# Two of the four weight sums of each gate/up pair of the second feed-forward made by an accumulating transfer

## The chip, the cores and the metric

The kernel runs on one core of a Trainium2 chip. The core has TensorE (PE in the profile; PEld is its weight load), VectorE (DVE), ScalarE (ACT), GpSimd (POOL) and SyncE (SP). Each takes its own list of instructions in a fixed order and waits on semaphores that others raise. Transfers between HBM and the on-chip memory are issued here from the lists of SyncE and GpSimd, and they run on 16 DMA engines that both share. The metric is the time of one execution on the device, in microseconds (us).

## The reference

One layer on 512 tokens of width 1024, all in float32: a SwiGLU feed-forward of width 2816, a merge of two token mixers (dilated attention and a gated linear recurrence), and a second SwiGLU feed-forward, each with an RMS norm before and after it. What matters here is the second feed-forward:

```
def swiglu(x, w_gate, w_up, w_down):
    return (jax.nn.silu(x @ w_gate) * (x @ w_up)) @ w_down
...
f = swiglu(rms_norm(h, ffn2_norm_pre[l]), ffn2_w_gate[l], ffn2_w_up[l], ffn2_w_down[l])
h = h + 0.5 * rms_norm(f, ffn2_norm_post[l])
```

## The kernel before

**Precision.** Every float32 operand is split into a high and a low part (`split`: ScalarE copies the rounded value, L302; VectorE subtracts it from the original, L303). A product is then three matmuls: high by high, high by low, low by high.

**Seven products instead of eight.** The 22 blocks of 128 gate and 128 up columns are numbered f. Those with f of 3 and more in the second feed-forward treat gate and up together as a two by two block matrix and multiply it with a two by two split of the activations in Strassen's manner, with seven products p1 to p7 instead of eight. The weights come as four pieces u0, u1, g0 and g1 of 128 rows by 512. `w_forms` makes four sums from them on VectorE: s2 = u0 + u1 (L691), s1 = s2 + g0 (L692), u0 + g0 (L693) and s1 + g1 (L696). Then it splits four tiles: a holds g0 and g1 (p1, p2), b holds s1 and s2 (p6, p5), c holds u0 + g0 and u1 (p7, p4), and d holds the last sum (p3).

**Order of the products.** Pairs 3 and 4 go through `seven` (copies on line L836), whose products follow each other as p1, p2, p6, p5, p7, p4, p3. Its accumulators are read out on the way: p1 is copied out (c1 below) before p6 accumulates on top of it, and that sum is copied out (c6) before p7 accumulates on top of that. The gate output of the first half (g0 below, L841) is read on VectorE before p4 reuses its bank. From pair 5 on, `seven_on` takes p1, p5, p6, p2, p7, p3, p4 (copies on L743). One product is 12 matmuls.

**Order of the whole.** `ffn_order` prepares the weights of pair f + 1 ahead of the products of pair f (`prep`, with a priority raised by AHEAD = 100). Between pairs it places parts of the down product (`prepd` for its weights, `down7` for its matmuls, L1043 to L1045), which is done in seven products too. A planner decides the order of the list of each engine from priorities and its own costs. Once built, the lists are fixed, and an instruction that waits holds up everything behind it in its list.

**Buffers.** Raw weights land by SyncE (L242) in a ring of four tiles of 512 KB (`raw`). Split weights use four tiles (`w8`) and two small ones (`w4`). The sums s1 and s2 share one tile under the tag `s`, of which there are two. Just ahead of the first pair both `s` tiles hold differences of the activations (`ts`, L667 and L668). The first of these is free once p5's activation form is split from it (`big<-ts`). The second is changed in place later (L673), and is free once p4's form is split from it (also `big<-ts`).

```
            DVE.tensor_add(s2, u0, u1)
            DVE.tensor_add(s1, s2, g0)
            DVE.tensor_add(u0, u0, g0)
            a, b, c, d = w8(), w8(), w8(), w4()
            split(a[:, 0, :], a[:, 1, :], gr)
            DVE.tensor_add(g1, s1, g1)
            split(b[:, 0, :], b[:, 1, :], s12.rearrange("p s c -> p (s c)"))
            split(c[:, 0, :], c[:, 1, :], ur)
            split(d[:, 0, :], d[:, 1, :], g1)
```

Of the kernel before, what the change touches and what calls it, by code (L numbers as in the profile page):

```python
# [10 lines left out]
F32 = mybir.dt.float32  # L11
F32R = mybir.dt.float32r
AF = mybir.ActivationFunctionType
ALU = mybir.AluOpType
AX = mybir.AxisListType

P = 128
T = 512
D = 1024
KC = D // P  # L20
NF = 22
FF_PARTS = ((0, 4), (4, 8), (8, 12), (12, 16), (16, 22))
NSTD = {1: 6, 2: 3}

SEVEN = range(4)
STEPS_AT = {1: ((6, 7, 7, 8), range(9, 13), range(13, 17), range(17, 21)),
# [5 lines left out]
RAW_W = 1024  # L32
# [3 lines left out]
AHEAD = 100  # L36
# [29 lines left out]
def ffn_order(n):  # L66

    order = [("std", f) for f in range(NSTD[n])]  # L70
    after = {}
# [3 lines left out]
    ready = False  # L75
    for f in range(NSTD[n], NF):
        if not ready:
# [83 lines left out]
def stream_groups():  # L161

    groups, cur, w = [], [], 0
    for key, width in stream_plan():
        if w + width > RAW_W or (cur and cur[0][0][0] == "start"):
            groups.append(cur)
            cur, w = [], 0
        cur.append((key, w, width))
        w += width
    groups.append(cur)  # L170
    return groups
# [12 lines left out]
def hybrid_layer(ctx: ExitStack, tc: tile.TileContext, xT: bass.AP, xN: bass.AP, wst: bass.AP,  # L184
                 first: bass.AP, rows: bass.AP, consts: bass.AP, bias: bass.AP, out: bass.AP):
    nc = tc.nc
    DVE, ACT, PE = nc.vector, nc.scalar, nc.tensor
# [3 lines left out]
    wpool = ctx.enter_context(tc.tile_pool(name="wpool", bufs=4))  # L191
# [39 lines left out]
    groups = stream_groups()  # L231
    state = {"g": 0, "i": 0, "off": 0, "raw": None, "ahead": AHEAD, "split": None}
# [21 lines left out]
    def raw_two(key, dst=None):  # L254

        return [raw_of(key + (n,), None if dst is None else dst[:, i * RAW_W:(i + 1) * RAW_W])
                for i, n in enumerate(("lo", "hi"))]

    def fetch(key, slot=None, ahead=0):

        with tc.high_priority(offset=ahead if slot else state["ahead"]):
            src = raw_of(key)
            w = src.shape[-1]
            t = slot() if slot else w8() if w > 512 else w4()
            split(t[:, 0, :w], t[:, 1, :w], src)
            return t[:, 0, :w], t[:, 1, :w]

    def w8():
        return wpool.tile([P, 2, 1024], F32R, name="w8", tag="w8", bufs=4)

    def w4():
        return wpool.tile([P, 2, 512], F32R, name="w4", tag="w4", bufs=2)
# [28 lines left out]
    def split(dh, dl, src):  # L301
        state["split"] = ACT.activation(dh, src, AF.Copy).ins  # L302
        state["low"] = DVE.tensor_sub(dl, src, dh.bitcast(F32)).ins  # L303
# [7 lines left out]
    def tmp(name):  # L311
        return tpool.tile([P, T], F32, name=name, tag="t")
# [17 lines left out]
    def gemm(ps, wt, x, sl=slice(0, T), ks=None):  # L330
        n = x.n
        a, b = k128(wt[0], n), k128(wt[1], n)
        for k in ks or range(n):
            mm3(ps, a[:, k, :], b[:, k, :], x.hi[k][:, sl], x.lo[k][:, sl], k == 0, k == n - 1)

    def gemm_first(keys, x, slots, then):


        wts = [fetch(k, None if i < 4 else slots.pop(0)) for i, k in enumerate(keys)]
        pss = [acc_ps() for _ in keys]  # L340
        for sl in HALVES:
            for i, (wt, ps) in enumerate(zip(wts, pss)):
                for k in range(x.n):
                    mm3(ps[:, sl], k128(wt[0])[:, k, :], k128(wt[1])[:, k, :], x.hi[k][:, sl],
                        x.lo[k][:, sl], k == 0, k == x.n - 1)
                if sl.start == 0:
                    for f in then.get(i + 1, ()):
                        f()
        return pss
# [95 lines left out]
    def gains(pool, *ids):  # L445

        t = pool.tile([P, 2, D], F32, name="gains", tag="wd", bufs=1)
        for j, i in enumerate(ids):
            nc.gpsimd.dma_start(t[:, j, :], bass.AP(tensor=rows.tensor, offset=rows.offset + i * D,
                                                    ap=[[0, P], [1, D]]))  # L450
        return t[:, 0, :], t[:, 1, :]
# [229 lines left out]

    spool = [None]

    def w_forms(key):

        with tc.high_priority(offset=AHEAD):
            ur, gr = raw_two(key)
            u0, u1, g0, g1 = (r[:, i * 512:(i + 1) * 512] for r in (ur, gr) for i in range(2))
            s12 = spool[0].tile([P, 2, 512], F32, name="s12", tag="s", bufs=2)
            s1, s2 = s12[:, 0, :], s12[:, 1, :]  # L690
# [9 lines that stand above are left out]
            lo, hi = slice(0, 512), slice(512, 1024)  # L700
            return {"p1": a[:, :, lo], "p2": a[:, :, hi], "p6": b[:, :, lo], "p5": b[:, :, hi],
                    "p7": c[:, :, lo], "p4": c[:, :, hi], "p3": d}
# [156 lines left out]
    def ffn(n, x, r, forms_x, apool, pss):  # L859
# [70 lines left out]
        def std_out(psg, psu, f):  # L930

            g = tmp("g")
            if r is None:
                ACT.activation(g, psg, AF.Silu)
                into(f, lambda dst, v: DVE.tensor_mul(dst, v(psu), v(g)))
                return
            u = tmp("u0")
            DVE.tensor_mul(g, psg, r)
            ACT.activation(g, g, AF.Silu)
            DVE.tensor_mul(u, psu, r)  # L940
            into(f, lambda dst, v: DVE.tensor_mul(dst, v(u), v(g)))
# [124 lines left out]

        keys = [(w, n, i) for i in range(NSTD[n]) for w in ("gate", "up")]
        forms = {}
        for ev in ffn_order(n):
            if ev[0] == "std":  # L1070
                j = ev[1]
                while len(pss) < 2 * j + 2:
                    pss.append(acc_ps())
                    gemm(pss[-1], fetch(keys[len(pss) - 1]), x)
                with tc.high_priority(offset=EVAC if j == NSTD[n] - 1 else 0):
                    std_out(pss[2 * j], pss[2 * j + 1], j)

                for step in steps[j:] if j == min(NSTD[n], 4) - 1 else steps[j:j + 1]:
                    step()
            elif ev[0] == "prep":  # L1080
                forms[ev[1]] = w_forms(("gu", n, ev[1]))
            elif ev[0] == "prepd":
                forms[ev[1:]] = d_forms(*ev[1:])
            elif ev[0] == "seeds":
                for g in groups(ev[2])[:3]:
                    seed(ev[1], *g)
            elif ev[0] == "down7":
                down7(*ev[1:], forms.pop(ev[1:]))
            else:
                prod(ev[1], forms.pop(ev[1]))  # L1090
# [9 lines left out]
    def spare(pool):  # L1100

        def of(t):
            return t[:, 0:4, :].rearrange("p (s k) t -> p s (k t)", s=2)

        return {"e": lambda: of(pool.tile([P, 8, T], F32R, name="act", tag="e", bufs=1)),
                "tt": lambda: of(pool.tile([P, 4, T], F32R, name="act", tag="tt", bufs=1)),
                "xf": lambda: of(pool.tile([P, 4, T], F32R, name="xf", tag="xf", bufs=4)),
                "tx": lambda: tx_slot(pool).rearrange("p s k t -> p s (k t)")}
# [15 lines left out]
    for k in range(KC):  # L1124
        wh, wl, raw = wts[k]
# [77 lines left out]
    with ExitStack() as mx:  # L1203
# [129 lines left out]
        def first_forms():  # L1333
            forms[order[0]] = w_forms(order[0])
# [5 lines left out]
        def pair_of(key):  # L1340

            i = order.index(key)
            if i + 1 < len(order):
                forms[order[i + 1]] = w_forms(order[i + 1])
            return forms.pop(key)
# [149 lines left out]
        for c in range(0, KC, 2):  # L1495
            g, u = tmp("g"), tmp("u")
# [12 lines left out]
    with ExitStack() as mx:  # L1509
# [183 lines left out]
        for c in range(KC):  # L1693
            if c < 3:
                ps = pss[c]
            else:
# [17 lines left out]
                 {(1, 3): lambda: (bd2.turn(0), bd2.turn(1))})  # L1714
    keys = [(w, 2, i) for i in range(NSTD[2]) for w in ("gate", "up")]
    pss = gemm_first(keys[:NFIRST], u2, [spare(ap2)["tx"]],
# [5 lines left out]
    grow5, _ = gains(ap2, 4)  # L1722
# [138 lines left out]
```

## Time and profile before

| what | value |
|---|---|
| median of 3 runs | 1209.24 us (1208.63 to 1209.45) |
| the profiled execution's own time | 1209.61 us |
| its span, first to last instruction | 1207.8 us |
| TensorE busy over the span | 1198.6 us (99%) |
| VectorE busy over the span | 1033.3 us (86%) |
| ScalarE busy over the span | 831.8 us (69%) |
| GpSimd busy over the span | 26.1 us (2%) |
| mean granted TensorE clock | 0.999 |
| pairs of the second feed-forward, from the first product of pair 3 | 898.55 us to about 1165 us |

All engine times in the text count from the start of the span of the profiled execution. A row of the timeline gives start, duration, engine, line, operation, and out<-in; behind it in brackets stands how long the engine had been idle before it, and what ended that. Matmuls overlap in their records: a matmul of 256 columns is shown as 0.28 us long, but the next one starts 0.12 us later. So a product of 12 matmuls takes 1.44 us. Transfers are shown with the time from issue to landing.

### The profile page before, as it was taken

Reading aid. Unit: us, or ns where it says so; the run is one execution under the profiler, and the core shown is the slowest. Engines: PE = TensorE matmul, PEld = TensorE weight load, DVE = VectorE, ACT = ScalarE, POOL = GpSimd, SP = SyncE. Lnnn points to the kernel's source line nnn. Section 1 sums busy time; section 2 is a strip of 40 time slices with the busy share of each in tenths; the row PEclk is TensorE's granted clock in tenths of the full one; section 3 lists DMA queues with packets and bytes.
Section 4 is the critical chain, followed back from the end, with each engine's and each line's share of the span. In section 5 each row is a group of like instructions: output and inputs, shape, how many; then the busy total and the mean of one; then the engine's idle time right before and its main releaser. Section 6 shows DMA issues by size and latency. Waiting matters only on the chain.

```text
span 1207.8 us, 18850 instructions
## 1 busy us (share of the span) xinstructions
PE 1198.6 (99%) x7222; PEld 1070.1 (89%) x7222; DVE 1033.3 (86%) x1626; ACT 831.8 (69%) x1447; POOL 26.1 (2%) x51
## 2 busy tenths in 40 slices
PE   9999999999999999999999999999999999999997
PEld 8889999999888888888888888888899999999996
DVE  7999888989689899999868999774799888889964
ACT  6566787887566576777736988734566687778763
POOL 0000000000011000000000000000100000000000
PEclk9999999999999999999999999999999999999999
DMA  7224343434725232222323532235443333333441
GB/s 267 88 92 139 120 139 109 137 117 150 250 106 154 71 101 91 89 87 80 122 67 110 176 121 88 88 107 189 140 142 121 121 125 117 128 120 126 125 173 70
DMA packets 45819, 149.77 MB, mean 124 GB/s; under 512 B 5152, under 2 KB 8608, under 8 KB 45728
## 3 DMA queue, kind: packets, MB, share of 16 engines
q1 hardware_dynamic: 38160, 131.09, 32.9%
q0 software_dynamic: 7280, 17.30, 4.3%
q8 instruction: 56, 0.92, 0.3%
q14 instruction: 35, 0.29, 0.1%
q10 hardware_dynamic: 288, 0.17, 0.0%
HBM read 138.06 MB, written 6.29 MB: 120 GB/s over the span
## 4 chain that ended last, share of the span: by engine, by line
PE 92%; DVE 4%; DMA 2%; ACT 1%; issue 1%; DVEq 0%; ACTq 0%
PE acc L779 10%; PE acc L729 9%; PE acc L731 9%; PE acc L730 9%; PE acc L315 7%; PE acc L317 7%; PE acc L316 7%; PE acc L780 5%; PE aux L1043 4%; PE aux L1044 4%; PE aux L1045 4%; PE acc L433 2%; PE acc L432 2%; PE acc L431 2%; DVE w L303 2%; DMA raw<-in_w 2%
## 5 line engine op out<-in xcount | busy, mean ns | idle before, releaser
L303 DVE TENSOR_TENSOR w<-raw,w 128x1024 fp32r<-128x1024 f32 (+1 forms) x272 | 296.9, 1097 | 32.2 <-ACT w L302 31.4
L302 ACT ACTIVATE w<-raw 128x1024 fp32r<-128x1024 f32 (+1 forms) x272 | 259.5, 958 | 90.0 <-PE acc L317 48.2
L729 PE MATMUL acc<-big,w 128*128 128x256 f32 x860 | 243.6, 283 | 0.0
L731 PE MATMUL acc<-big,w 128*128 128x256 f32 x860 | 243.4, 283 | 0.0
L730 PE MATMUL acc<-big,w 128*128 128x256 f32 x860 | 243.3, 283 | 0.0
L729 PEld LDWEIGHTS acc<-big,w 128*128 128x128 f32 x860 | 164.8, 192 | 1.8
L730 PEld LDWEIGHTS acc<-big,w 128*128 128x128 f32 x860 | 164.8, 192 | 1.5
L731 PEld LDWEIGHTS acc<-big,w 128*128 128x128 f32 x860 | 164.8, 192 | 0.0
L779 PE MATMUL acc<-big,w 128*128 128x512 f32 x380 | 136.5, 398 | 0.0
L780 PE MATMUL acc<-big,w 128*128 128x256 f32 x380 | 107.5, 283 | 0.0
L1043 PE MATMUL aux<-w,xf 128*128 128x512 f32 x224 | 87.3, 392 | 0.6 <-ACT w L302 0.6
L1044 PE MATMUL aux<-w,xf 128*128 128x512 f32 x224 | 87.5, 391 | 0.0
L1045 PE MATMUL aux<-w,xf 128*128 128x512 f32 x224 | 87.2, 389 | 0.0
L779 PEld LDWEIGHTS acc<-big,w 128*128 128x128 f32 x380 | 71.4, 188 | 16.0 <-ACT acc L784 0.2
L780 PEld LDWEIGHTS acc<-big,w 128*128 128x128 f32 x380 | 71.7, 189 | 0.3
L303 DVE TENSOR_TENSOR w<-s,w 128x1024 fp32r<-128x1024 f32 x51 | 62.2, 1220 | 3.2 <-ACT w L302 2.7
L315 PE MATMUL acc<-xf,w 128*128 128x512 f32 (+1 forms) x168 | 59.2, 354 | 0.0
L316 PE MATMUL acc<-xf,w 128*128 128x512 f32 (+1 forms) x168 | 58.7, 350 | 0.0
L317 PE MATMUL acc<-xf,w 128*128 128x512 f32 (+1 forms) x168 | 58.5, 349 | 0.0
L302 ACT ACTIVATE w<-s 128x1024 fp32r<-128x1024 f32 x51 | 53.9, 1057 | 6.2 <-PE acc L731 3.0
L779 PE MATMUL acc<-rb,w 128*128 128x512 f32 x152 | 55.5, 397 | 0.0
L743 ACT ACTIVATE c<-acc 128x256 f32<-128x256 f32 x68 | 25.8, 383 | 35.3 <-PE acc L731 35.3
(458 smaller groups left out, 2919.5 us busy)
## 6 DMA issues: line engine op xcount, KB each, us to landing
raw<-in_w SPq DMA_DIRECT2D x232, 512.0 KB, 3.5
big<-xf POOLq DMA_DIRECT2D x6, 512.0 KB, 3.3
gains<-in_rows POOLq DMA_DIRECT2D x5, 512.0 KB, 5.4
h<-in_x SPq DMA_DIRECT2D x8, 256.0 KB, 5.1
h<-in_xn POOLq DMA_DIRECT2D x4, 512.0 KB, 6.7
kept_m<-h POOLq DMA_DIRECT2D x4, 512.0 KB, 2.9
vals<-in_w SPq DMA_DIRECT2D x4, 512.0 KB, 6.0
h<-kept_m POOLq DMA_DIRECT2D x4, 512.0 KB, 6.2
```

What stands on the lines that cost most here:

```text
L302: state["split"] = ACT.activation(dh, src, AF.Copy).ins
L303: state["low"] = DVE.tensor_sub(dl, src, dh.bitcast(F32)).ins
L315: PE.matmul(ps, wh, xh, start=first, stop=False)
L316: PE.matmul(ps, wh, xl, start=False, stop=False)
L317: PE.matmul(ps, wl, xh, start=False, stop=last)
L729: PE.matmul(ps, wh, xh, start=start and k == 0, stop=False, skip_group_check=True)
L730: PE.matmul(ps, wh, xl, start=False, stop=False, skip_group_check=True)
L731: PE.matmul(ps, wl, xh, start=False, stop=k == 3, skip_group_check=True)
L779: PE.matmul(part, wh, at(BOTH, k), start=start and k == 0, stop=False, skip_group_check=True)
L780: PE.matmul(cross, wl, at(0, k), start=False, stop=k == 3, skip_group_check=True)
L1043: PE.matmul(ps, xh, wh, start=first and j == 0, stop=False, skip_group_check=True)
L1044: PE.matmul(ps, xh, wl, start=False, stop=False, skip_group_check=True)
```

## The change

For the pairs of the second feed-forward, the raw pieces come in another way. GpSimd's list issues two transfers for each pair. The first writes u0 twice into the tile s. The second adds u1 to the first half and g0 to the second half while it writes (accumulate), and it is issued once the first has landed. So s holds u0 + u1 and u0 + g0 without VectorE. SyncE's list issues the gate half (512 KB) and u1 alone (256 KB). VectorE makes only the other two sums, into the raw tiles. The tiles are regrouped for it: b now holds p5 and p7, and c holds p6 and p4. Other users of `w_forms` are unchanged.

```
+def SUMMED(key):
+    return key[:2] == ("gu", 2)
...
+    def raw_sums(key):
+
+        (g, i), off = (state["g"], state["i"]), state["off"]
+        assert i == 0 and groups[g] == [(key + ("lo",), 0, RAW_W)] and groups[g + 1] == [(key + ("hi",), 0, RAW_W)]
+
+        def at(o, *dims):
+            return bass.AP(tensor=wst.tensor, offset=wst.offset + off + o, ap=[[RAW_W, P], *dims, [1, T]])
+
+        s = spool[0].tile([P, 2, T], F32, name="s12", tag="s", bufs=2)
+        nc.gpsimd.dma_start(s, at(0, [0, 2]))
+        nc.gpsimd.dma_start(s, at(T, [P * RAW_W - T, 2]), accum_op=ALU.add)
+        gr, ur = (wpool.tile([P, RAW_W], F32, name="raw", tag="raw", bufs=4) for _ in range(2))
+        nc.sync.dma_start(gr, bass.AP(tensor=wst.tensor, offset=wst.offset + off + P * RAW_W,
+                                      ap=[[RAW_W, P], [1, RAW_W]]))
+        nc.sync.dma_start(ur[:, T:], at(T))
+        state["g"], state["off"] = g + 2, off + 2 * P * RAW_W
+        return s, ur, gr
+
+    def w_forms_summed(key):
+
+        with tc.high_priority(offset=AHEAD):
+            s, ur, gr = raw_sums(key)
+            a, b, c, d = w8(), w8(), w8(), w4()
+            split(a[:, 0, :], a[:, 1, :], gr)
+            DVE.tensor_add(ur[:, :T], s[:, 0, :], gr[:, :T])
+            split(b[:, 0, :], b[:, 1, :], s.rearrange("p s c -> p (s c)"))
+            split(c[:, 0, :], c[:, 1, :], ur)
+            DVE.tensor_add(gr[:, T:], ur[:, :T], gr[:, T:])
+            split(d[:, 0, :], d[:, 1, :], gr[:, T:])
+            lo, hi = slice(0, T), slice(T, D)
+            return {"p1": a[:, :, lo], "p2": a[:, :, hi], "p5": b[:, :, lo], "p7": b[:, :, hi],
+                    "p6": c[:, :, lo], "p4": c[:, :, hi], "p3": d}
+
     def w_forms(key):
 
+        if SUMMED(key):
+            return w_forms_summed(key)
         with tc.high_priority(offset=AHEAD):
             ur, gr = raw_two(key)
```

## The prediction

> **What bounds the kernel now.** I read the page first, then one window over the pairs, then what TensorE waited for, and last the timelines around the first pairs. On the page, line 1 gives the busy time of each engine and line 4 the chain of work that ended last:
>
> ```profile
> span 1207.8 us, 18850 instructions
> ...
> PE 1198.6 (99%) x7222; PEld 1070.1 (89%) x7222; DVE 1033.3 (86%) x1626; ACT 831.8 (69%) x1447; POOL 26.1 (2%) x51
> ...
> PE 92%; DVE 4%; DMA 2%; ACT 1%; issue 1%; DVEq 0%; ACTq 0%
> ```
>
> That is an average over stages. The window from the first product of pair 3 to the end of the pairs (its row), and TensorE's waits from 850 us on (the only one that the view lists):
>
> ```profile
> core 0: us, PE busy (x) PEld busy (x) DVE busy (x) ACT busy (x) POOL busy (x), PEclk, DMA share, GB/s
> 898.55:1165.00 266.45, 265.83 (x1904) 251.35 (x1903) 232.59 (x310) 198.59 (x337) 2.66 (x5) 1.00 0.39 126
> ```
>
> ```profile
> PE aux L1043 <- ACT w L302: 0.6, 3, 0.2
> ```
>
> The reader is to see that TensorE is idle for 266.45 − 265.83 = 0.6 us in the stage that the change touches, at a granted clock of 1.00. VectorE is busy for 87% of it, but nothing that matters waits for it. So the change can win 0.6 us at most. What it can lose depends on new waits.
>
> **What it removes.** These groups, taken from the pairs alone, are the work on the sums:
>
> ```profile
> L691 DVE TENSOR_TENSOR s<-raw x19: 677/683/694, 884.5 to 1146.1; 128x512 f32<-128x512 f32 x19
> L693 DVE TENSOR_TENSOR raw<-raw x19: 678/684/686, 886.3 to 1148.7; 128x512 f32<-128x512 f32 x19
> L302 ACT ACTIVATE w<-s x19: 1043/1062/1067, 887.5 to 1153.6; 128x1024 fp32r<-128x1024 f32 x19
> L303 DVE TENSOR_TENSOR w<-s,w x19: 1211/1217/1226, 888.8 to 1154.7; 128x1024 fp32r<-128x1024 f32 x19
> ```
>
> Of four additions, two (L691, L693) leave VectorE: 19 × (0.683 + 0.684) = 26.0 us. They lie beside TensorE, which waits 0.6 us. I take −0.6 us, with bounds −0.6 and 0.
>
> **What it adds in transfers.** SyncE still issues two transfers per pair, one of them halved. GpSimd issues 38 more. Its list does 2.66 us of work in the window, and at 0.53 to 0.75 us for an issue (rows below) the 38 cost it 20 to 29 us that nobody needs. The latency of the two transfers, which follow each other, is what counts. No accumulating transfer is in the trace. These are the nearest rows: a lone 512 KB transfer from HBM on GpSimd's queue in this stage, and the four of `h`, which run in pairs beside each other:
>
> ```profile
> L449 POOL DMA_DIRECT2D gains<-in_rows x1: 541/541/541, 1140.6 to 1140.6; - x1
> ...
> DMA to landing us min/median/max: 3.8/3.8/3.8
> ```
>
> ```profile
> L1721 POOL DMA_DIRECT2D h<-kept x4: 528/532/541, 1160.3 to 1162.6; - x4
> ...
> DMA to landing us min/median/max: 3.6/5.6/6.4
> ```
>
> The first, plain transfer is like the lone one: 3.8 us. The accumulating one writes the same 512 KB, so it takes at least 3.8 us. From above I take three such passes (read, read, write, with nothing overlapping): 11.4 us. Between these I choose 6.4 us, the slowest of the transfers that shared the engines with another, because an accumulation brings two streams to each engine. With 0.1 us for the semaphore between them, the chain S is 3.8 + 0.1 + 6.4 = 10.3 us, with ends 7.7 and 15.3 us.
>
> The Trainium skill has a mechanism for this price: Collectives: The Full Stack, section "The bandwidth ceiling: the fold count and why AG ≠ RS ≠ AR", says that a reduction is slower than a copy because it needs two source reads, and not because of its addition. With the fit in DMA: Bandwidth & Descriptors, section "Anatomy of one DMA — SWDGE (gpsimd) path" (2.0 us plus bytes over 436 GB/s), this gives an estimate of 3.2 us for the plain transfer and 4.4 us for the accumulating one, and S would be 7.7 us. The lone transfer of the trace took 3.8 us, 0.6 us over that fit, and no run here shows an accumulating one yet.
>
> **Where S stands open: pair 3.** Both `s` tiles are taken by `ts` at first. VectorE frees one when it has split p5's form, and GpSimd still has its last copy to issue. The rows behind those are VectorE's list up to the first products, with pair 4's split of b later on:
>
> ```profile
> 882.14 0.74 POOL L655 DMA_DIRECT2D big<-xf  x1 [2.96 <-issue]
> ```
>
> ```profile
> 880.95 1.22 DVE L303 TENSOR_TENSOR big<-ts,big 128x1024 fp32r<-128x1024 f32 x1
> ...
> 885.71 0.68 DVE L692 TENSOR_TENSOR s<-s,raw 128x512 f32<-128x512 f32 x1
> 886.31 0.68 DVE L693 TENSOR_TENSOR raw<-raw 128x512 f32<-128x512 f32 x1
> ...
> 888.77 1.22 DVE L303 TENSOR_TENSOR w<-s,w 128x1024 fp32r<-128x1024 f32 x1
> ...
> 899.60 1.21 DVE L303 TENSOR_TENSOR big<-ts,big 128x1024 fp32r<-128x1024 f32 x1
> 900.73 1.22 DVE L303 TENSOR_TENSOR w<-raw,w 128x1024 fp32r<-128x1024 f32 x1
> 901.87 0.42 DVE L841 TENSOR_TENSOR g<-acc,c 128x256 f32<-128x256 f32 x1
> ```
>
> The first transfer is issued at 882.14 + 0.74 = 882.9, and s(3) is ready at 882.9 + 10.3 = 893.2. VectorE's list, where each add starts 0.60 after the one before, stands at s(3)'s first user from about 886 on. These 7 us of waiting cost TensorE nothing, because it is still in the products ahead of the pairs. VectorE then does two adds and the low part of b: 893.2 + 0.6 + 0.6 + 1.22 = 895.6.
>
> **Pair 4: the first loss.** In the built order s(4) takes the tile of s(3), since p4's form holds the other one. It is issued at 895.7 and ready at 906.0. ScalarE's list in both kernels has c1, then the split of pair 4's b, then c6 of pair 3:
>
> ```profile
> 900.18 0.38 ACT L836 ACTIVATE c<-acc 128x256 f32<-128x256 f32 x1 [0.33 <-PE acc L731]
> 901.68 1.06 ACT L302 ACTIVATE w<-s 128x1024 fp32r<-128x1024 f32 x1 [1.12 <-PE acc L731]
> ...
> 903.45 0.36 ACT L836 ACTIVATE c<-acc 128x256 f32<-128x256 f32 x1
> ```
>
> ```profile
> 898.55 0.28 PE L729 MATMUL acc<-big,w 128*128 128x256 f32 x1
> ...
> 904.30 0.28 PE L729 MATMUL acc<-big,w 128*128 128x256 f32 x1
> ...
> 908.62 0.28 PE L729 MATMUL acc<-big,w 128*128 128x256 f32 x1
> ```
>
> The three starts are those of p1 and p7 of pair 3 and p1 of pair 4; a product takes (904.30 − 898.55) / 4 = 1.44 us. p7 needs c6. The split now starts at 906.0 and not at 901.68, c6 ends at 906.0 + 1.06 + 0.36 = 907.4, and p7 starts at 907.5: 3.2 us late. Behind s(4)'s add in VectorE's list stand the low part of pair 4's a, p4's form and g0 of pair 3. They end at 906.0 + 0.6 + 1.14 + 1.14 + 0.42 = 909.3, while p4 could start at 907.5 + 1.44 = 908.95: 0.4 more. Sum 3.6 us.
>
> **Pair 5: the second loss.** s(5) takes the other tile when p4's form is split, at 906.0 + 0.6 + 1.14 + 1.22 = 909.0. It is issued at 909.1 and ready at 919.4. (In GpSimd's list the plain transfer of s(6) stands between its two; it waits for the split of pair 4's b, which comes next on VectorE, and adds nothing.) In VectorE's new list s(5)'s first add stands ahead of the product of gate and up of pair 3, g0 of pair 4 and one difference. ScalarE's split of those activations stands ahead of c6 of pair 4:
>
> ```profile
> 910.95 0.68 DVE L968 SCALAR_TENSOR_TENSOR tt<-g,u 128x512 f32<-128x512 f32 x1
> 911.77 0.42 DVE L841 TENSOR_TENSOR g<-acc,c 128x256 f32<-128x256 f32 x1
> 912.12 0.68 DVE L919 TENSOR_TENSOR tt<-tt 128x512 f32<-128x512 f32 x1
> ```
>
> ```profile
> 912.83 0.63 ACT L302 ACTIVATE xf<-tt 128x512 fp32r<-128x512 f32 x1
> 913.37 0.37 ACT L836 ACTIVATE c<-acc 128x256 f32<-128x256 f32 x1
> ```
>
> So that c6 ends at 919.4 + 0.6 + 0.6 + 0.35 + 0.68 + 0.63 + 0.37 = 922.6. Pair 4 starts at 908.62 + 3.6 = 912.2 and could start its p7 at 912.2 + 4 × 1.44 = 918.0: 4.6 us late. Together 3.6 + 4.6 = 8.2 us, and in general 3 S − 22.7 us, since S enters three times ahead of that point.
>
> **From pair 6 on: nothing.** One pair later in steady state, in VectorE's list, and the copy of p1 that dates its pair:
>
> ```profile
> 1025.04 1.22 DVE L303 TENSOR_TENSOR w<-s,w 128x1024 fp32r<-128x1024 f32 x1
> ...
> 1027.84 1.22 DVE L303 TENSOR_TENSOR w<-raw,w 128x1024 fp32r<-128x1024 f32 x1
> ...
> 1040.66 1.22 DVE L303 TENSOR_TENSOR w<-s,w 128x1024 fp32r<-128x1024 f32 x1
> ```
>
> ```profile
> 1030.49 0.39 ACT L743 ACTIVATE acc<-acc 128x256 f32<-128x256 f32 x1
> ```
>
> An `s` tile is free after b's split, and the add for the pair after next stands just behind the next such split: 1040.66 − 1025.04 = 15.6 us, against S = 10.3. This is the cover; without it each of 17 pairs would wait for the excess.
>
> **The regrouping.** p6 moves into c, so c is due at the third product and not the fifth. Here c ends at 1027.84 + 1.22 = 1029.1, and its pair starts at 1030.49 − 1.44 = 1029.05. The due time falls from 1034.8 to 1029.05 + 2.88 = 1031.9, so 2.8 us of cover remain, and VectorE has less to do: 0 us (bounds 0 and 0.5 a pair). b holds its slot to the fifth product instead of the third, which is still sooner than c's: 0. The list of TensorE differs only near pair 20, where one group of the down product begins sooner: 0, the same matmuls.
>
> **Sum.** 1209.61 (the profiled execution) − 0.6 + 8.2 = 1217.2. That execution lies 0.4 us over the median of the runs shown, so I predict 1217 us.
>
> **Rivals.** (1) The transfers are hidden: no change. 3 S − 22.7 is 0.4 at S = 7.7, which gives 1209.4, and it stays within 0.2% (2.4 us, about what a measurement of this kernel can tell from no change) up to S = 8.6, an accumulation of 4.7 us. The lone 3.8 us speaks for it, the 5.6 and 6.4 of shared transfers against it. By the skill's two-reads rule this rival is the outcome, and my S is too long. (2) The accumulation is a slow unit's work: at S = 15.3 the start alone costs 23.2 us, 1232 us. Above 15.6 each further 1 us of S adds up to 17 us in the steady pairs. No row of the trace speaks for such a price, and none excludes it. (3) Faster: VectorE's 26 us come back because it is the hidden bound of the pairs. That would need more than 2.4 us of TensorE waits in the window, where the rows show 0.6. At best 1209.0 comes out.
>
> **Chances.** My case (S from 8.6 to 13, 1212 to 1226 us) 0.53; the hidden one 0.20; the slow one 0.23, half of it above 1235; faster 0.04. So slower 0.76, same 0.20, faster 0.04. The range from 1209 to 1235 leaves out some 0.15; my own case's range is 1212 to 1226.
>
> **What would show it.** TensorE idle in two places, ahead of p7 of pair 3 and of p7 of pair 4, near 904 and 914 us, and next to nothing after 930. ScalarE's split of pair 4's b would wait for an accumulating transfer that lands near 906. Transfers of `s` should show 3.8 and 6.4 us. VectorE's busy time should fall by 26 us. I am wrong if the accumulation takes under 4.7 us or over 9, or if TensorE waits once per pair up to the end.

## The result, and the profile after

The changed kernel takes 1247.57 us (1242.74 to 1250.96 over four runs) against 1209.35 us in the same comparison: a ratio of 1.0313, 95% interval 1.0275 to 1.0352. That is 38.2 us more, where I had predicted 7.8 more and at most 26. The direction was right, the size was not.

The profiled execution is the fastest of the four, 1242.74 us, so the trace explains 33.2 us of span (1241.0 − 1207.8) and not all of the median's 38.2. The busy time of each engine on its page of the profile:

```profile
PE 1206.0 (97%) x7222; PEld 1074.3 (87%) x7222; DVE 1011.2 (81%) x1588; ACT 832.0 (67%) x1447; POOL 62.9 (5%) x89
```

VectorE loses 22.1 us of busy time. TensorE does the same 7222 matmuls, but it is busy for 7.4 us longer. What it waited for from 850 us on (behind the colon stand the sum in us, how often, and the longest):

```profile
PE acc L770 <- ACT c L877: 13.9, 3, 9.9
PE aux L1084 <- ACT aux L1073: 9.4, 4, 2.9
PE aux L1084 <- ACT facc L1089: 1.5, 1, 1.5
PE aux L1084 <- ACT w L308: 1.4, 4, 0.8
PE aux L1085 <- DVE w L309: 0.6, 1, 0.6
PE acc L770 <- DVE g L882: 0.2, 1, 0.2
```

The sum is 27.0 us, where it was 0.6 before. 27.0 − 0.6 + 7.4 = 33.8, which is the 33.2 us of the span but for 0.6. So three things have to be found: the waits of pairs 3 and 4 (L770, 14.1 us), the waits of the down product (L1084 and L1085, 12.9 us) and the longer busy time of TensorE.

**The first pairs.** GpSimd's list in the timeline, up to pair 6 (two rows each for s(3) and s(4), then the first transfers of s(5) and s(6), and the second one of s(5)):

```profile
881.45 0.71 POOL L699 DMA_DIRECT2D s<-in_w  x1 [0.55 <-DVE big L309]
885.95 1.24 POOL L700 DMA_DIRECT2D s<-in_w  x1 [3.80 <-DMA s<-in_w]
895.33 0.73 POOL L699 DMA_DIRECT2D s<-in_w  x1 [8.14 <-DVE w L309]
899.91 1.21 POOL L700 DMA_DIRECT2D s<-in_w  x1 [3.85 <-DMA s<-in_w]
909.81 0.72 POOL L699 DMA_DIRECT2D s<-in_w  x1 [8.69 <-DVE g L882]
911.02 0.73 POOL L699 DMA_DIRECT2D s<-in_w  x1 [0.48 <-DVE w L309]
914.62 1.24 POOL L700 DMA_DIRECT2D s<-in_w  x1 [2.87 <-DMA s<-in_w]
```

VectorE's first use of s(3), s(4) and s(5):

```profile
892.42 0.69 DVE L714 TENSOR_TENSOR raw<-s,raw 128x512 f32<-128x512 f32 x1 [6.20 <-DMA s<-in_w]
...
906.19 0.69 DVE L714 TENSOR_TENSOR raw<-s,raw 128x512 f32<-128x512 f32 x1 [2.20 <-DMA s<-in_w]
...
925.16 0.69 DVE L714 TENSOR_TENSOR raw<-s,raw 128x512 f32<-128x512 f32 x1 [8.39 <-issue]
```

And TensorE, the rows with the three longest idle times ahead of them, in p6 and p7 of pair 3 and p7 of pair 4:

```profile
902.06 0.39 PE L770 MATMUL acc<-tx,w 128*128 128x256 f32 x1 [1.52 <-ACT c L877]
907.65 0.39 PE L770 MATMUL acc<-big,w 128*128 128x256 f32 x1 [2.45 <-ACT c L877]
...
928.37 0.58 PE L770 MATMUL acc<-big,w 128*128 128x256 f32 x1 [9.94 <-ACT c L877]
```

The first of the three, 1.52 us, still comes from s(3). ScalarE's split of p4's form waits for VectorE, which stood still for 6.20 us ahead of s(3)'s first use and worked without a pause since. The copy c1 stands behind that split:

```profile
899.74 1.06 ACT L308 ACTIVATE big<-ts 128x1024 fp32r<-128x1024 f32 x1 [1.70 <-DVE ts L679]
...
901.65 0.37 ACT L877 ACTIVATE c<-acc 128x256 f32<-128x256 f32 x1
```

S is 892.42 − 881.45 = 11.0 us for s(3) and 906.19 − 895.33 = 10.9 for s(4), but 925.16 − 909.81 = 15.3 for s(5). Its accumulation alone takes 925.16 − 914.62 = 10.5 us. For its first 2.6 us it runs beside the plain transfer of s(6), which landed 6.2 us after its issue at 911.02. For most of the rest it runs beside two raw loads, issued at 915.00 and 916.46, which took 7.5 and 8.8 us. In windows of 2 us the DMA share, the last column but one, is 0.91 and 1.08 while it runs:

```profile
918.00:920.00 2.00, 0.43 (x4) 0.23 (x2) 0.00 (x0) 0.39 (x1) 0.00 (x0) 1.00 0.91 202
920.00:922.00 2.00, 0.00 (x0) 0.00 (x0) 0.00 (x0) 0.00 (x0) 0.00 (x0) 1.00 1.08 265
922.00:924.00 2.00, 0.00 (x0) 0.00 (x0) 0.00 (x0) 0.00 (x0) 0.00 (x0) 0.84 0.48 164
...
932.00:934.00 2.00, 2.00 (x13) 2.00 (x13) 1.48 (x3) 1.79 (x3) 0.00 (x0) 0.60 0.00 0
```

**The clock.** The column ahead of the DMA share is the granted TensorE clock. TensorE's last matmul ends at 918.4. Some 5 us later the clock falls to 0.50, and it stays there until about 933.6 (0.60 is a mean over 1.6 us at 0.50 and 0.4 at 1.00), that is for 5 us after the matmuls have begun again at 928.4. In these 5 us TensorE is busy at half speed.

**The down product.** From pair 6 on TensorE does not wait for gate or up, but five times for more than 1 us ahead of a step of the down product (up to 956.37, 1020.25, 1084.16, 1147.57 and 1180.07). VectorE's waits name what is behind the first four, which end 5.7 to 6.7 us after the start of the add that waited:

```profile
DVE raw L1036 <- DMA raw<-in_w: 28.6, 4, 8.1
```

L1036 is the add u0 + u1 of the down product's third step (L995 before, where it waited 0.9 us in two times). One of the four, in VectorE's list of the changed kernel:

```profile
1068.12 1.22 DVE L309 TENSOR_TENSOR w<-raw,w 128x1024 fp32r<-128x1024 f32 x1 [0.53 <-ACT w L308]
1077.46 1.23 DVE L1036 TENSOR_TENSOR raw<-raw 128x1024 f32<-128x1024 f32 x1 [8.11 <-DMA raw<-in_w]
```

and the same place in the kernel before:

```profile
1046.74 1.22 DVE L303 TENSOR_TENSOR w<-raw,w 128x1024 fp32r<-128x1024 f32 x1
1047.88 0.69 DVE L693 TENSOR_TENSOR raw<-raw 128x512 f32<-128x512 f32 x1
1050.19 1.22 DVE L303 TENSOR_TENSOR w<-sum,w 128x1024 fp32r<-128x1024 f32 x1 [1.63 <-ACT w L302]
1051.72 1.23 DVE L995 TENSOR_TENSOR raw<-raw 128x1024 f32<-128x1024 f32 x1 [0.30 <-DMA raw<-in_w]
```

The load that this add needs goes into the raw tile that the split in the first row of each fence frees: the second issue of SyncE ends at 1069.70, just behind that split's end at 1069.34. Before, an add and the split of the other sum stood between the split and its use, and the load landed in 3.6 us. Now the use is VectorE's next instruction, and the load takes 8.0 us. It runs beside an accumulating transfer (the experiments below show that a plain one does nearly the same):

```profile
1067.02 2.68 SPq L248 DMA_DIRECT2D raw<-in_w  x2
...
1068.86 1.19 POOL L700 DMA_DIRECT2D s<-in_w  x1 [4.38 <-DMA s<-in_w]
```

While VectorE stands still, everything behind it is late, and ScalarE with it. The rows of ScalarE, then two of TensorE's waits, this one and the one four pairs earlier:

```profile
1080.52 0.42 ACT L992 ACTIVATE g<-g 128x256 f32<-128x256 f32 x1 [5.68 <-DVE g L991]
...
1083.51 0.59 ACT L1073 ACTIVATE aux<-ea 128x512 f32<-128x512 f32 x1
```

```profile
1020.25 0.50 PE L1084 MATMUL aux<-w,xf 128*128 128x512 f32 x1 [2.86 <-ACT aux L1073]
...
1084.16 0.79 PE L1084 MATMUL aux<-w,xf 128*128 128x512 f32 x1 [2.86 <-ACT aux L1073]
```

Of the 8.1 us, 2.86 reach TensorE at 1084.16 as waiting, and the clock falls again, as the windows around this place show:

```profile
1080.00:1082.00 2.00, 1.30 (x5) 0.73 (x5) 2.00 (x5) 1.39 (x3) 0.00 (x0) 1.00 0.63 234
1082.00:1084.00 2.00, 0.00 (x0) 0.00 (x0) 2.00 (x4) 2.00 (x4) 0.00 (x0) 0.95 0.00 0
1084.00:1086.00 2.00, 1.84 (x4) 1.49 (x5) 2.00 (x5) 2.00 (x5) 0.74 (x1) 0.50 0.23 51
1086.00:1088.00 2.00, 2.00 (x12) 1.78 (x11) 1.56 (x2) 1.42 (x4) 0.00 (x0) 0.70 0.87 292
```

The gap of the same length at 1020.25 has no such fall: the granted clock is 1.00 in every window of 2 us from 1016 to 1024. The gap of 1.84 us that ends at 1147.57 has one, from about 1148.6 to 1152.0. So the length of a gap alone does not decide it.

The fifth wait, 1.87 us up to 1180.07, has another cause. In the last pair VectorE comes to the first use of `s` at 1168.7, only 7.3 us after the first of its two transfers was issued at 1161.38, and it waits for the accumulation. ScalarE's copy for the down product stands behind a split that is late by it:

```profile
1173.84 0.69 DVE L714 TENSOR_TENSOR raw<-s,raw 128x512 f32<-128x512 f32 x1 [5.13 <-DMA s<-in_w]
```

### The profile page after: what moved, and what is told of

It reads as the page before. It is cut to its first block, busy times and chain, and to the rows that moved or that the text cites. A ratio compares the mean times of both kernels' runs of the same rounds, so it can differ in the third digit from the quotient of the medians.

```text
span 1241.0 us, 18879 instructions
## 1 busy us (share of the span) xinstructions
PE 1206.0 (97%) x7222; PEld 1074.3 (87%) x7222; DVE 1011.2 (81%) x1588; ACT 832.0 (67%) x1447; POOL 62.9 (5%) x89
## 5 line engine op out<-in xcount | busy, mean ns | idle before, releaser
L770 PE MATMUL acc<-big,w 128*128 128x256 f32 x860 | 245.9, 286 | 12.6 <-ACT c L877 12.4
L770 PEld LDWEIGHTS acc<-big,w 128*128 128x128 f32 x860 | 166.9, 194 | 14.9 <-ACT c L877 12.8
L1084 PE MATMUL aux<-w,xf 128*128 128x512 f32 x224 | 88.5, 398 | 12.3 <-ACT aux L1073 9.4
L1085 PE MATMUL aux<-w,xf 128*128 128x512 f32 x224 | 88.5, 395 | 0.6 <-DVE w L309 0.6
L1086 PE MATMUL aux<-w,xf 128*128 128x512 f32 x224 | 88.1, 393 | 0.0
L309 DVE TENSOR_TENSOR w<-s,w 128x1024 fp32r<-128x1024 f32 x51 | 62.2, 1220 | 3.3 <-ACT w L308 2.8
L1084 PEld LDWEIGHTS aux<-w,xf 128*128 128x128 f32 x224 | 42.1, 189 | 22.9 <-ACT aux L1073 11.1
```

The costliest lines, as they stand in the source:

```text
L770: PE.matmul(ps, wh, xh, start=start and k == 0, stop=False, skip_group_check=True)
L1084: PE.matmul(ps, xh, wh, start=first and j == 0, stop=False, skip_group_check=True)
L1085: PE.matmul(ps, xh, wl, start=False, stop=False, skip_group_check=True)
L1086: PE.matmul(ps, xl, wh, start=False, stop=j == 1, skip_group_check=True)
```

## The experiments

In each comparison the kernel before ran on the same chip, at 1209.44 to 1209.76 us. "More" is counted from there.

**Is it the accumulation, or a second transfer at all?** In the first kernel the second transfer is plain (the diff), so it overwrites u0 instead of adding to it. In the second kernel its line is left out altogether, and with it both additions.

```
-        nc.gpsimd.dma_start(s, at(T, [P * RAW_W - T, 2]), accum_op=ALU.add)
+        nc.gpsimd.dma_start(s, at(T, [P * RAW_W - T, 2]))
```

> The second transfer of each pair writes u1 and g0 over the first instead of adding them; bytes, issues and the order of every engine's list stay as in the changed kernel. It leaves the two sums of u0 out. Theory (the price of the accumulation: an accumulating transfer takes 6.3 us alone and up to 10.5 us beside others, and it slows the raw loads beside it from 3.5 to 8 us): the chain of two falls from 11 to about 9 us, the start costs 3 x 9.1 - 22.7 = 5 us, the waits of 8 us for raw weights once in four pairs (L1036) fall under 4 us and hide; 1212 to 1220 us. Rival (bytes and issues on GpSimd's queue, or the new order of the lists, whatever the operation): within 8 us of the changed kernel, 1240 to 1250 us.

> The second transfer of each pair is left out, so the tile holds u0 twice; the additions of u1 and g0 are missing. Theory (chain length and the traffic of the accumulation): with a chain of 4.5 us nothing waits at the start and raw loads are as fast as before: 1208 to 1212 us. Rival (the regrouping, with c due at the third product, and the order that the planner made of it): the time stays above 1225 us.

Measured: 1228.5 us with the plain one (1.0156, interval 1.0131 to 1.018) and 1213.43 without it (1.0032, 1.0019 to 1.0044). So of the 38.2 us, some 19 go with the accumulation, 15 with a second transfer of that size, and 4 are there with one transfer alone. Both times are misses, the first by far: my theory had the plain kernel at 1220 at most, and the one without the second transfer at 1212. VectorE's wait at the down step's add, in the plain kernel, tells why:

```profile
DVE raw L1036 <- DMA raw<-in_w: 27.3, 4, 7.5
```

It is nearly as long as with the accumulation (28.6), and TensorE still waits 6.8 us in sum for L1073. The start is as the prediction's formula has it: it loses 5.9 us, and the three chains as measured, 8.5, 9.1 and 11.1 us, give 28.7 − 22.7 = 6.0.

**Which pairs cost it?** `SUMMED` is cut to the pairs from 6 on (the diff), or to the pairs 3 to 5 (with `< 6` in its place).

```
-    return key[:2] == ("gu", 2)
+    return key[:2] == ("gu", 2) and key[2] >= 6
```

> Pairs 3, 4 and 5 make their sums on VectorE as before, pairs 6 to 21 by the accumulating transfer. Theory (two separate losses: the serial start, and raw loads slowed in the steady pairs, each with lost clock behind it): the 14 us of TensorE waits before 930 us and some 4 us of lost clock behind them go, the steady loss of 13 us plus its clock stays: 1220 to 1232 us. Rival (all of the loss begins at the start and is only carried on): 1208 to 1213 us.

> Only pairs 3, 4 and 5 use the accumulating transfer, pairs 6 to 21 make their sums on VectorE as before. Theory (the loss adds up from a start and a steady part; the run without the start lost 18 us of 38): 1225 to 1233 us, with the TensorE waits of 14 us before 930 us and next to none later. Rival (the parts are not independent: the start only hurts because the steady pairs cannot make up for it): 1210 to 1220 us.

Measured: 1227.67 us (1.014, 1.0101 to 1.018) from pair 6 on, 18.2 more; 1225.97 us (1.0134, 1.0119 to 1.0149) up to pair 5, 16.3 more. Together they are 34.5 of the 38.2. The runs of the first kernel lie 10.9 us apart, and its interval reaches from 12.2 to 21.8 us; its trace is of the slowest run, 1231.24 us. So the pairs for which I had "nothing" carry about half. The largest item of TensorE's waits in the first kernel (14.4 us in all) and then in the second (11.7):

```profile
PE aux L1084 <- ACT aux L1073: 11.1, 4, 2.9
```

```profile
PE acc L770 <- ACT c L877: 11.0, 3, 6.7
```

The two do not mix: the L770 waits belong to the start, the L1084 waits to the later pairs. TensorE's busy time is 1206.5 us in the one and 1203.5 in the other, against 1198.6 before, and in both the granted clock falls to 0.50 around some of the gaps.

**Is it the regrouping and the new lists?** VectorE makes all four sums again, but with the tiles grouped as in the change (b holds p5 and p7, c holds p6 and p4).

```
+            new = key[:2] == ("gu", 2)
+            DVE.tensor_add(s1 if new else s2, u0, u1)
+            if new:
+                DVE.tensor_add(s2, u0, g0)
+                DVE.tensor_add(u0, s1, g0)
```

> All four sums on VectorE and all loads by SyncE as before, but the tiles grouped as in the changed kernel (b for p5 and p7, c for p6 and p4), in the second feed-forward only. Theory (grouping costs nothing, as predicted): 1208 to 1211 us. Rival (c due two products sooner is late, or the planner's new order is worse): 1213 us or more, with TensorE waiting for c once per pair.

Measured: 1211.8 us (1.0019, 1.001 to 1.0029), 2.3 more, a little above what I expected. VectorE's list comes out in another order here. So the regrouping and what the planner makes of it is not quite free, but it is no large part.

**Is it the start's chain through two `s` tiles?** The `s` of every third pair, pair 3 among them, goes into a spare tile, so that three tiles take turns.

```
-        s = spool[0].tile([P, 2, T], F32, name="s12", tag="s", bufs=2)
+        s = (npool.tile([P, 2, T], F32, name="s12", tag="nr", bufs=1) if key[2] % 3 == 0
+             else spool[0].tile([P, 2, T], F32, name="s12", tag="s", bufs=2))
...
```

> The changed kernel with a third tile for the sums: every third pair (3, 6, 9 and so on) uses 4 KB per partition that only the first feed-forward used, so the sums of pair 3 need not wait for the activation differences, and those of pair 4 not for pair 3. Theory (the start is lost to a chain of transfers through one tile): most of the 14 us of waits before 930 us goes, with the lost clock behind it; the steady loss of some 18 us stays: 1226 to 1238 us. Rival (the accumulation is late at the start whatever tile it uses): above 1242 us.

Measured: 1231.39 us (1.017, 1.0153 to 1.0187), 16.2 less than the changed kernel. TensorE waits once at the start and not three times, and VectorE's wait for the raw load is as in the changed kernel (28.2 us, four times, the longest 7.9):

```profile
PE acc L771 <- ACT c L878: 5.5, 1, 5.5
```

**Is it the raw tile that the down step waits for?** The second piece of that step gets a tile of its own outside the ring, so that its load can go earlier. First in the changed kernel, then in the one that accumulates from pair 6 on.

```
-                raw = [raw_of(("dq", n, a, q)) for q in SEVEN_RAW[i]]
+                own = npool.tile([P, 2, T], F32, name="own", tag="nr", bufs=1).rearrange("p s c -> p (s c)") if n == 2 and i == 2 else None
+                raw = [raw_of(("dq", n, a, q), own if k else None) for k, q in enumerate(SEVEN_RAW[i])]
...
```

> The changed kernel, with the second of the two down-weight pieces that are added to each other once in four pairs (L1036) loaded into a tile of its own instead of the ring of four raw tiles. The start is as in the changed kernel. Theory (the steady loss is one load, issued when VectorE frees its tile and needed by VectorE's next instruction, which takes 8 us instead of 3.5 beside the accumulation): waits of L1036 fall from 8 us to nearly 0, and the time to 1226 to 1236 us. Rival (the steady loss comes from the traffic or from the clock in general): above 1240 us.

> Both removed: accumulation from pair 6 on only, and the second down-weight piece in a tile of its own. Theory (the two losses are all there is): 1209 to 1216 us. Rival (a loss that goes with the accumulation itself, per pair): 1220 us or more.

Measured: 1229.57 us (1.0163, 1.0148 to 1.0178) and 1213.37 us (1.0028, 1.0018 to 1.0039), that is 18.0 and 14.3 us less than without the tile. VectorE's wait at that add in the second kernel, and the largest item of TensorE's waits (4.3 us in all):

```profile
DVE raw L1037 <- DMA raw<-in_w: 9.0, 4, 2.5
```

```profile
PE aux L1085 <- ACT aux L1074: 2.9, 1, 2.9
```

The wait falls from 25.4 to 9.0 us, though not to nearly nothing, as I had it. TensorE's waits fall from 14.4 to 4.3, its busy time from 1206.5 to 1198.9, and the mean granted clock rises from 0.994 to 1.000. So the steady part is for the most part one shared raw tile and the clock that falls in its wake: without them 16 accumulating pairs cost 3.7 us. The 2.9 us of TensorE's that are left in one piece have the other cause: they follow a wait of VectorE's of 6.66 us for the last pair's `s`. The sum of the two cures also fits: what is left of the changed kernel with the own tile, 19.9 us, is the start's 16.3 plus these 3.7. I had only one spare tile, so both cures in one kernel were not tried. The planner also moved some of VectorE's, ScalarE's and SyncE's rows for the new tile, so the gain is that of the tile together with these moves. The add itself did not move away from the split: around 1049 us in the second kernel it still stands right behind one, with the same rows ahead of it as at 1077 us in the changed kernel. But its second load is issued at 1050.84, for the next use some 60 us later. Moving only the add in VectorE's list was not tried.

**What does the traffic cost by itself?** The kernel before keeps all its sums on VectorE and issues two more transfers for each pair. In the first attempt a small VectorE copy paced them. In the second kernel of the two the second transfer is plain.

```
...
+                DVE.tensor_copy(x[:, 0, 0:1], u0[:, 0:1])
+                nc.gpsimd.dma_start(x, at(0, [0, 2]))
+                nc.gpsimd.dma_start(x, at(T, [P * RAW_W - T, 2]), accum_op=ALU.add)
...
```

> The kernel before, with all its work, and beside it the two transfers per pair into a spare tile that nobody reads, started when VectorE has copied one element per row of the pair's raw weights (19 small copies). It shows the traffic of the accumulation by itself. Theory (the traffic is only a loss where VectorE's next instruction needs the load): raw loads that land beside an accumulation take up to 8 us, some waits of VectorE for raw weights grow, TensorE waits little: 1209 to 1216 us. Rival (the traffic alone costs what the changed kernel lost in the steady pairs): 1222 us or more.

> The same with a plain second transfer. Theory (an accumulation loads the engines like more than one plain transfer): raw loads land sooner than beside the accumulation, 1209 to 1213 us, and not above the run with the accumulation. Rival (a transfer is a transfer): the same landings of raw loads and the same time in both.

Measured: 1249.03 us (1.0319) and 1226.35 us (1.0143). Both lie above my ranges, and the trace shows that the experiment was at fault. The pacing copy itself waited until the earlier transfers into `x` had landed, and held up VectorE's list. In the first kernel:

```profile
DVE x L697 <- DMA x<-in_w: 26.2, 8, 5.6
```

So these two say nothing of the traffic alone. They show once more what one waiting VectorE instruction costs. The second attempt has no further instruction on VectorE; only GpSimd's list waits. The first transfer copies the tile of sums, the second reads the pair's weights from HBM again, and not the raw tiles. As before, the second kernel has a plain transfer in place of the accumulating one.

```
+                x = npool.tile([P, 2, T], F32, name="x12", tag="nr", bufs=1)
+                nc.gpsimd.dma_start(x, s12)
+                nc.gpsimd.dma_start(x, bass.AP(tensor=wst.tensor, offset=wst.offset + state["off"] - 2 * P * RAW_W + T,
+                                               ap=[[RAW_W, P], [P * RAW_W - T, 2], [1, T]]), accum_op=ALU.add)
...
```

> The kernel before, all of its sums still on VectorE, and beside each gate/up pair of the second feed-forward two further 512 KB transfers of GpSimd's, the second accumulating, from a tile in SBUF and from the pair's raw tiles into a spare tile that nobody reads. Only GpSimd's list waits for them. Theory (a transfer beside the raw loads makes them late, and TensorE pays only where VectorE's next instruction needs that load): raw loads land in up to about 8 us beside the accumulation, as in the changed kernel, but the down step's u0 + u1 stands three adds behind the split and waits a few us at most; time 1209 to 1216. Rival (the traffic alone is what costs, wherever the adds stand): VectorE waits for raw 20 us or more in sum and the time is 1222 or more.

> The same with the second transfer plain, no accumulation; lists otherwise the same. Theory: raw loads land in up to about 7 us, time 1209 to 1212. Rival (accumulation occupies the DMA engines no more than a copy): the raw landings and the time are those of the accumulating variant within 1 us.

Measured: 1220.62 us (1.0097, 1.0077 to 1.0117), 10.9 more, and 1215.4 us (1.0044, 1.0029 to 1.0059), 5.6 more. My theory's times were too low in both. By its time the accumulating variant lies between my theory and the rival; VectorE's waits for raw are 21.4 us in sum, as the rival said, but they are spread over many adds, and the down step's add waits as little as the theory said:

```profile
DVE s L692 <- DMA raw<-in_w: 11.1, 9, 2.7
...
DVE raw L1000 <- DMA raw<-in_w: 4.3, 4, 1.7
```

So traffic costs by itself, though this kernel has more of it than the changed one, which loads u1 alone and not the whole up half. That an accumulation is no more than a copy is refuted. The page of the profile has a row for GpSimd's queue: packets, MB, and the time that its packets took, as a share of 16 engines' span. Here it is for the kernel before, for two plain transfers a pair, and for one plain and one accumulating:

```profile
q0 software_dynamic: 7280, 17.30, 4.3%
```

```profile
q0 software_dynamic: 12752, 37.23, 9.1%
```

```profile
q0 software_dynamic: 15184, 37.23, 11.8%
```

Of spans of 1207.8, 1213.8 and 1215.9 us these are 51.9, 110.5 and 143.5 us of all 16 engines. A plain transfer takes (110.5 − 51.9) / 38 = 1.54 us of them, and an accumulation in its place (143.5 − 110.5) / 19 = 1.74 more. So by this estimate it holds the engines for 3.28 / 1.54 = 2.1 times as long as a copy; the two kinds of plain transfer, one from on-chip memory and one from HBM, are taken as equal. The bytes are counted the same, but the accumulation has 272 packets, where a plain transfer has 144.

## Why the prediction was wrong in size

- **"TensorE is idle for 0.6 us", gain at most 0.6.** Right. VectorE's busy time fell by 22.1 us, and nothing came back from it. The 26.0 us were 38 durations of 0.68; the records of neighbouring adds overlap, and at the 0.60 from start to start they are 22.8.
- **S = 10.3 us.** Nearly right for transfers that run without much beside them: 11.0 and 10.9. The plain transfer was the part that I had too short (4.5 us from its issue to the next issue, against 3.8 + 0.1); the accumulating one took 6.3 to 6.5, against 6.4. By the two-source-reads rule of the Trainium skill (Collectives: The Full Stack, "The bandwidth ceiling: the fold count and why AG ≠ RS ≠ AR") my estimate had been 4.4 us. The trace agrees in direction, with about twice the packets and engine time of a copy, but the measured 6.3 us are more than this estimate.
- **Pair 3, nothing lost.** Right in time, as s(3) is used at 892.42, where I had 893.2, but the path was not free. I followed s(3) to the low part of b alone. VectorE's work behind it also delays the copy c1, and p6 starts 1.52 us late. The sum is no larger for it, since p7 waits for s(4) in any case.
- **Pair 4, 3.6 us.** Nearly right: ScalarE's split of s(4) holds up the copy c6, and g0 is late for p4. TensorE is 1.52 + 2.45 + 0.19 = 4.16 us late by then.
- **Pair 5, 4.6 us.** Right in mechanism, mis-sized: 9.94 us. The term is S of s(5). I took the same S for each chain, but this accumulation ran beside the end of s(6)'s plain transfer and two raw loads, and took 10.5 us. In the kernel that accumulates only up to pair 5, with no transfer for s(6), it still takes 8.6 us (915.30 to 923.91), so s(6) is not the main part of it. With S as measured, 11.0 + 10.9 + 15.3 − 22.7 = 14.5. The chain began 1.4 us sooner than I had it (881.45 against 882.9), and pair 3 1.0 us sooner (897.51 against 898.55), which takes off 0.4: 14.1 us, as measured. I had S = 15.3 as an end of the range, but only as the price of a slow unit for all three.
- **"From pair 6 on: nothing".** This is the step that failed. I compared S with the 15.6 us until an `s` tile is needed again, read at one place for all pairs. It holds but for the last pair, where the cover is 7.3 us, VectorE waits 5.13 us for `s`, and TensorE 1.87. The larger part is two things that I left out: the transfers lengthen SyncE's loads on the same DMA engines, and in the planner's new list the down step's add stands straight behind the split that frees its raw tile. The order of VectorE's list in the changed kernel was known in advance, and the prediction reads in it only the users of `s`. Cost: 18.2 us, of which the own tile takes back 14.3.
- **The term that wasn't there: the clock.** I counted waits at their length. Around some of them the clock is at 0.50 for some microseconds, and TensorE's busy time grows by 7.4 us, a fifth of the loss. It is so from about 923.4 to 933.6 (the gap of 9.94 us), from about 1083.8 to 1087.2 (the second gap of 2.86 us) and from about 1148.6 to 1152.0 (the gap of 1.84 us). TensorE works in 5.2, 3.0 and 3.4 us of these, and half of their sum, 5.8 us, is my estimate of what the clock took; the other 1.6 us I can't place. The Trainium skill has a rule for it (TensorE: Matmul & The Clock Gate, "Part 1: The HAM clock gate"): half rate after an idle window of about 3.4 us, full rate after about as long a busy one. The trace agrees for the long gap, where the clock fell 4.9 us after the last matmul and rose 5.2 us after the next one. It does not for the shorter gaps: two of 2.86 and 1.84 us brought the fall, and one of 2.86 us did not. What decides between them is not shown here.
- **The regrouping, 0.** It cost 2.3 us (1.2 to 3.5 by the interval).
- **What I had named as proof against me** came true in one point of two: not an accumulation over 9 us as a rule (the median of the 19 landed in 7.8), but waits up to the end, once per down step and not once per pair.

What stays open: 38.2 us is 3.7 more than the sum of the two halves, measured apart. That lies within the intervals, and the lists of the two halves differ from the whole's too; no run tells this apart. Which of the transfers beside s(5)'s accumulation lengthened it, and by how much, is not measured either. The runs of the changed kernel lie 8.2 us apart, against 1.3 before, and I have one trace, of the fastest.

## What to carry to other kernels

Moving work from an idle-enough engine to the DMA engines is no gift: ask which other loads run on them at that time, and what the first instruction is that needs one of those loads. In a fixed list, a late load costs little as long as other work stands between the instruction that frees its tile and the one that uses it. When work is taken out of a list, look at every tile whose reload was hidden by that work, and not only at the tiles that the change touches. And where TensorE is the bound, count on a waiting time that costs more than its length: here 27.0 us of waits came with 7.4 us of longer busy time, most of it at half speed, though not every gap brought it.

## What the hardware showed that I had not expected

- An accumulating transfer of 512 KB took 6.3 to 6.5 us with little beside it and up to 10.5 us beside others, and its issue holds GpSimd for 1.2 us where a plain one's holds it for 0.74. This row groups the 19 accumulating issues, with the shortest, the median and the longest time of one in ns:

```profile
L700 POOL DMA_DIRECT2D s<-in_w x19: 1181/1195/1242, 886.0 to 1166.0; - x19
...
DMA to landing us min/median/max: 5.8/7.8/10.5
```

- Transfers of GpSimd's slow the loads of SyncE's queue, whether they accumulate or not. From 895 to 1165 us the 512 KB raw loads landed in 3.5 us (median) in the kernel before, in 4.2 with the first transfer alone, in 4.6 with a plain second one and in 4.5 with the accumulating one. The longest raw load took 5.0, 4.9, 7.3 and 8.8 us.
- The granted clock fell to 0.50 with a gap as short as 1.84 us, and stayed at 1.00 through one of 2.86 us.
